# Neighbourhood attention scores as three rounded products of keys and queries that are split on arrival

## The chip, the cores and the metric

One core of one Trainium2 chip runs the whole kernel as one program. The metric is device time in microseconds. Three runs of the kernel before took 1056.29, 1057.15 and 1058.18 us; the median is 1057.15 us.

## The reference

One layer of an encoder over 2048 tokens, which form a grid of 32 rows by 64 columns, with 1024 features and 16 heads of 64. The tokens are normalised (RMS), projected to queries, keys, values and a gate, and each token attends to a window of 8 rows by 16 columns around it, with a learned bias for each relative position. Gated outputs are projected, added to the input and normalised again.

```python
h = rmsnorm(x, norm_0)
q, k, v, gate = jnp.split(h @ w_in_0, 4, axis=-1)
# each row r, blocks of 16 query columns, 8 key rows and 32 key columns around them:
s = jnp.einsum('bnqhd,bknjhd->bhnqkj', qr, kr).astype(jnp.float32) * scale
s = jnp.where(col_valid[None, None], s + bias[None], NEG_INF)
p = jax.nn.softmax(s.reshape(B, H, nb, NA_QBLOCK, kh * NA_KBLOCK), axis=-1)
o = jnp.einsum('bhnqkj,bknjhd->bnqhd', p, vr)
x = x + (o * silu(gate)) @ w_out_0
return rmsnorm(x, norm_f)
```

All inputs are float32.

## The kernel before

The kernel first computes most projections (stages one and two, lines 570 to 907), to about 582 us of the profile. Every one of their products is made of three matmuls with operands in a rounded float32 format (F32R): an operand is split into a rounded high part, copied by ACT (ScalarE), and the remainder, subtracted by DVE (VectorE); the product is high x high + high x low + low x high, added up in PSUM.

Then the attention runs in 33 steps m (line 1429). A step's unit is a pair of heads p and a group T of eight query rows; `order` (line 933) has first the eight pairs with T = 0, then sixteen steps with T = 1 and 2, then eight with T = 3. The number of key rows of T = 0 to 3 is 11, 15, 15 and 12 (`KEY_ROWS`), so the key tile kt holds 704, 960, 960 or 768 columns of 64; the queries qt hold 512. The two heads of the pair lie in partitions 0 to 63 and 64 to 127.

The order of all instructions is written out by hand (`manual_schedule`), and every engine works through its own list in that order. One step m emits:

1. `begin` (line 1404) queues loads for later points of the step on SP (SyncE): the gate sgt for unit m-1 (`load_sg`, pool sp, two buffers), the values of unit m, the queries and keys of unit m+1 (`load_q`, `load_k`, two buffers each).
2. `feed(8)`: eight matmuls of what is left of the projections or, later, of the output projection (lines 379 to 383, 1346 to 1350). `feed` also emits stores and other work that has come due.
3. `normalise(2m-1)` (line 1044): a reciprocal on DVE (L1046), then the probabilities of half a unit are scaled, two tiles by GpSimd (L1055) and two by ACT (L1053).
4. One set of roots of finished output rows (`run_roots`, eight small DVE operations, L1248 to L1255), the splitting of rows for the output projection (`split_rows`, L1198 on ACT, L1199 on DVE) or of weights (`consume`, L189 and L190, L194 and L195), and the rest of the step's feed.
5. `turns(m-1)` (line 1078): PE (TensorE) transposes the probabilities of unit m-1 into six PSUM banks (L1112), and ACT and DVE copy three banks each to SBUF (tile pta, L1088).
6. `scores(2m)` and `scores(2m+1)` (line 1016): for each of four column groups and two heads one float32 matmul of queries and keys (L1027), DVE adds bias and mask from tile em and takes the row minimum (L1035), and ACT does Exp with the row sum (L1041).
7. `values(2m-2)`, `values(2m-1)` (line 1117): PE multiplies pta by the values into bank o (L1134), and DVE multiplies by the gate (L1140).

All PSUM tiles rotate through eight banks. In the first step there is nothing to normalise, and `feed(a * 0.6)` follows `feed(8)` directly.

A 128 x 128 tile `ones` is set by DVE at the start, copied by ACT into the rounded `onesr` (line 674), and read by one GpSimd instruction (line 1466) that only makes that engine wait for pta. `ident`, an identity matrix made by GpSimd, serves the transposes.

Of the kernel before, what the change touches and what calls it, by code (L numbers as in the profile page):

```python
# [10 lines left out]
F32 = mybir.dt.float32  # L11
F32R = mybir.dt.float32r
BF16 = mybir.dt.bfloat16
I32 = mybir.dt.int32
AF = mybir.ActivationFunctionType
OP = mybir.AluOpType
# [4 lines left out]
ROWS, GW, KH, KW = 32, 64, 8, 16  # L21
# [12 lines left out]
KEY_ROWS = [(0, 11), (4, 19), (12, 27), (20, 32)]  # L34
# [36 lines left out]
def build(ctx, tc, x, xr, xt, wg, rpb, last, w_out, n0, nf, masks, out):  # L71
    nc = tc.nc
# [8 lines left out]
    def pool(name, bufs):  # L81
        p = ctx.enter_context(tc.tile_pool(name=name, bufs=bufs))
        return lambda shape, dt, nm: p.tile(shape, dt, name=nm, tag=name)
# [3 lines left out]
    wp = pool("wp", 8)  # L87
    raw = pool("raw", 6)
    kp = pool("kp", 2)
    qp = pool("qp", 2)  # L90
    vp = pool("vp", 2)
    vhalf = []
# [4 lines left out]
            vhalf.extend((t[:, :512], t[:, 512:]))  # L97
        return vhalf.pop(0)

    sp = pool("sp", 2)  # L100
    xp = pool("xp", 8)
    mkp = pool("mkp", 1)
    pt = pool("pt", 1)
    mp = pool("mp", 10)
# [19 lines left out]
        nc.tensor.matmul(zp, z[:, :128], z, start=True, stop=True)  # L124
    ident = one.tile([128, 128], F32, name="ident")
    make_identity(nc, ident)
    ones = one.tile([128, 128], F32, name="ones")
    nc.vector.memset(ones, 1.0)
    onesr = one.tile([128, 128], F32R, name="onesr")
    rt = one.tile([128, 16], F32, name="rt")  # L130
    rth = one.tile([128, 8], F32, name="rth")
# [438 lines left out]
    def stage_one():  # L570
# [6 lines left out]
        land["x12"] = [kp([128, 960], F32, "land")[:, :512] for _ in range(2)] + [xp([128, 512], F32, "land") for _ in range(2)]  # L577
        sixth = sixths()
        land["x21"] = [spot[:, k] for k in range(3)] + [lp([128, 512], F32, "land")]
        slots = [(mp, 512)] * 8 + [(sp, 512)] * 2 + sixth[:2] + [(vh, 512)] * 4  # L580
        slots += sixth[2:] + [(mp, 512)] * 2 + [(qp, 512)] * 2

        def load(f, k):
# [87 lines left out]
        parts_ = slice(0, 256), slice(256, 512)  # L671
        load_v0(0, 0, 0, cols=parts_[0], by=nc.scalar)
        load_x(0, "x11", 0, land["x11"][0], parts_[0])
        nc.scalar.activation(onesr, ones, AF.Copy)
        load_v0(0, 1, 0, cols=parts_[0])
        load_x(0, "x11", 0, land["x11"][0], parts_[1])
        load_v0(0, 0, 0, cols=parts_[1])
# [120 lines left out]
    def stage_two():  # L798
# [3 lines left out]
        for k in range(4):  # L802
            load_x(2, "x22", k, x22[k])
        slots = {"T2": [(mp, 512)] * 8,
                 "T3": [(sp, 512)] * 2 + sixth[:5] + [(lp, 512)],
                 "T4": [(vh, 512)] * 4 + [(mp, 512)] * 2 + [sixth[5], (qp, 512)]}

        def also(n, i):
# [120 lines left out]


    KT, VT, QT, EM, SG, E = {}, {}, {}, {}, {}, {}
    LAST, stored_at = {}, {}
    order = [(p, 0) for p in range(NP)] + [(p, T) for p in range(NP) for T in (1, 2)] + [(p, 3) for p in range(NP)]
    pairs = [(p, T, (h, h + 1)) for p, T in order for h in (0, 2)]
# [9 lines left out]
    def load_k(p, T):  # L944
        r0, r1 = KEY_ROWS[T]
        n = (r1 - r0) * GW
        must(*[("k", p, c) for c in range(r0 // 8, (r1 + 7) // 8)])

        def keys():
            t = kp([128, 960], F32, "kt")  # L950
            KT[p, T] = t.rearrange("p (r c) -> p r c", c=GW)
            nc.sync.dma_start(t[:, :n], kd[p][:, r0 * GW:r1 * GW])

        return keys

    def load_q(p, T):
        must(("q", p, T))
# [58 lines left out]
    def scores(i, between=None):  # L1016
        p, T, cs = pairs[i]
        kt, qt = KT[p, T], QT[p, T]
        r0, r1 = KEY_ROWS[T]
        got = []  # L1020
        for C in cs:
            c0, c1 = KEY_COLS[C]
            qs = slice(C * 128, C * 128 + 128)
            pst = [bank((r1 - r0) * (c1 - c0), f"s{s}") for s in range(2)]
            for s in range(2):
                a = slice(s * 64, s * 64 + 64)
                nc.tensor.matmul(pst[s], qt[a, qs], kt[a, :r1 - r0, c0:c1].rearrange("p r (s c) -> p s r c", c=8), start=True, stop=True)  # L1027
            got.append((C, pst))
        ST[i] = st = tiny.tile([128, 12], F32, name="st")
        for j, (C, pst) in enumerate(got):  # L1030
            n = (r1 - r0) * width(C)
            X[i, C] = [xp([128, 512], F32, f"x{s}")[:, :n] for s in range(2)]
            for s in range(2):
                o = 2 * j + s
                nc.vector.tensor_tensor_reduce(X[i, C][s], pst[s], EM[p, ROW_TYPE[T], COL_TYPE[C], s], -1.0, 1e38,  # L1035
                                               OP.add, OP.min, st[:, o:o + 1])
            if between and j == 0:
                between()
            for s in range(2):
                o = 2 * j + s  # L1040
                nc.scalar.activation(X[i, C][s], X[i, C][s], AF.Exp, bias=st[:, o:o + 1], scale=-1.0,  # L1041
                                     accum_out=st[:, 4 + o:5 + o])
# [386 lines left out]
    for m in range(cycles + 1):  # L1429
        a = amount[m] - 8  # L1430
        begin(m)
        feed(8)
        if m:
            due_here = []
            quiet[0] = True
            if a < 12 and m > 8 and m % 2:
                normalise(2 * m - 1, True, lambda: due_here.append(split_rows() or consume(1, turn=True)))
            else:
                normalise(2 * m - 1, True)
            if a > 12:  # L1440
                run_roots()
            elif not rows_due():
                run_roots(1)
            for k in range(3):
                if m == 1 and k == 2:
                    pass
                elif a > 12 or not any(due_here) and (k < 1 or k < 2 and m > 8 and m % 2 == 0):
                    got = split_rows()
                    due_here.append(got)
                    if not got:  # L1450
                        consume(1, turn=True)
                    elif a < 12 and m % 2 == 0 and len(items) - state["used"] == 8:
                        feed(a * 0.2)
                        consume(1, turn=True)
                feed(a * 0.2)
        else:
            feed(a * 0.6)
        quiet[0] = False
        feed(a * 0.4, 8 if a > 12 else 4)
        sums = next_sums(m) == m + 1  # L1460
        if m:
            turns(m - 1)
            first_sums = m + 2 if m + 2 in pair_steps else m + 1 if sums and m + 1 not in pair_steps else None
            if first_sums:
                after = tiny.tile([128, 12], F32, name="st")
                nc.gpsimd.tensor_scalar(after[:88, 0:1], PT[m - 1][:88, 1, 0:1], ones[:88, 0:1], 1.0, op0=OP.mult, op1=OP.mult)
                tables(first_sums, 0, 1)
        if m == cycles:
            all_loads()
            feed(6)  # L1470
        else:
            scores(2 * m)
            if sums:
                tables(m + 1, 2)
            if m == 0:
                feed(first)
            scores(2 * m + 1, lambda: normalise(2 * m))
            if m == 0:
                consume(2, turn=True)
        if m:  # L1480
            values(2 * m - 2)
            values(2 * m - 1)
        runs[0] += 1
        for n in range(2, 24):
            if n < 8 and m == n - 2 or n == 8 and m == 5 or n in pair_steps and m == n - 3:
                for f in load_e(order[n][0], ROW_TYPE[order[n][1]], homes=accs if n >= 8 and n % 4 == 0 else None):
                    f()
        if m == 20:
            late_loads()
# [52 lines left out]
```

## Time and profile before

| | us |
|---|---|
| median of three runs | 1057.15 |
| lowest, highest | 1056.29, 1058.18 |
| span of the profiled execution | 1054.4 |
| PE busy | 1046.1 |
| DVE busy | 696.7 |
| ACT busy | 537.2 |
| GpSimd (POOL) busy | 252.0 |

The profile gives one execution by its span, from the first to the last instruction; no separate time of that execution is known, and the median of the runs lies 2.75 us above the span. A row of a group names the line, the engine, the operation, output and inputs, shapes and count; then the busy time, the mean duration of one in ns, and the idle time of the engine before such an instruction with what ended it. A row of a timeline begins with start and duration in us. Durations overlap a little with the next instruction on the same engine, so prices are better taken from one start to the next.

### The profile page before, as it was taken

The numbers are of one execution on the slowest core, as the hardware profiler recorded it, in microseconds if no ns is written. First come the engines' busy times: TensorE is split into PE (matmuls) and PEld (weight loads), VectorE is DVE, ScalarE is ACT, GpSimd is POOL, SyncE is SP. The second block draws the span as 40 slices with busy tenths as digits, with TensorE's granted clock in tenths as the row PEclk, the third lists the DMA queues.
The fourth block names the chain that finished last, engine by engine and source line by source line (L and its number), as shares of the span: only waits on it lengthen the run. The fifth ranks groups of instructions, "written<-read, shape, count | busy, mean of one in ns | idle before, by whom it ended". The sixth has DMA issues, their size and how long they took to land.

```text
span 1054.4 us, 20160 instructions
## 1 busy us (share of the span) xinstructions
PE 1046.1 (99%) x7316; PEld 858.8 (81%) x7316; DVE 696.7 (66%) x1570; ACT 537.2 (51%) x1260; POOL 252.0 (24%) x342
## 2 busy tenths in 40 slices
PE   9999999999999999999999999999999999999997
PEld 7888888887888888888888788888887888888886
DVE  5476667778897625555655766687777886667554
ACT  7645223443444334232332677688787865455422
POOL 0000322312211000000002467666665322112100
PEclk9999999999999999999999999999999999999999
DMA  9634444343635433333236777778777588775352
GB/s 320 219 100 118 132 150 136 120 144 120 187 119 154 121 100 93 116 110 121 90 110 211 219 232 235 219 252 281 243 237 217 184 277 272 245 233 183 120 166 80
DMA packets 120252, 184.19 MB, mean 175 GB/s; under 512 B 10776, under 2 KB 55064, under 8 KB 120152
## 3 DMA queue, kind: packets, MB, share of 16 engines
q1 hardware_dynamic: 119720, 182.50, 55.1%
q8 instruction: 57, 0.93, 0.4%
q10 hardware_dynamic: 432, 0.40, 0.1%
q14 instruction: 43, 0.35, 0.1%
HBM read 132.53 MB, written 50.33 MB: 173 GB/s over the span
## 4 chain that ended last, share of the span: by engine, by line
PE 96%; DVE 2%; issue 1%; ACT 1%; DMA 0%; SPq 0%; DVEq 0%; ACTq 0%
PE pp L435 36%; PE pv L559 17%; PE s L1027 8%; PE o L1134 8%; PE po L1346 6%; PE po L1348 5%; PE po L1350 5%; PE ph L1112 4%; PE pp L381 2%; PE pp L383 2%; PE pp L379 2%; DVE f L418 0%; DVE x L1035 0%; DMA raw<-in_wg_dram 0%; DVE raw L424 0%
## 5 line engine op out<-in xcount | busy, mean ns | idle before, releaser
L435 PE MATMUL pp<-h,f 128*128 128x512 f32 x672 | 217.4, 389 | 0.0
L1041 ACT ACTIVATE x<-x,st 128x360 f32<-128x360 f32 (+5 forms) x256 | 151.1, 592 | 23.0 <-DVE st L1035 23.0
L1055 POOL TENSOR_SCALAR x<-x,st 128x480 f32<-128x480 f32 (+5 forms) x192 | 111.7, 599 | 153.5 <-DVE st L1046 148.6
L435 PEld LDWEIGHTS pp<-h,f 128*128 128x128 f32 x672 | 126.2, 188 | 26.2
L435 PE MATMUL pp<-t,f 128*128 128x512 f32 x558 | 141.7, 389 | 0.1
L435 PE MATMUL pp<-l,f 128*128 128x512 f32 x336 | 130.7, 389 | 0.0
L1035 DVE CUSTOM_DVE_ANT_0 x<-s,em 128x360 f32<-128x360 f32 (+5 forms) x256 | 123.0, 535 | 0.5 <-PE s L1027 0.4
L435 PEld LDWEIGHTS pp<-t,f 128*128 128x128 f32 x558 | 104.7, 188 | 22.2 <-DVE u L448 0.6
L455 POOL TENSOR_TENSOR tmp<-tmp,rb 128x512 f32<-128x512 f32 x36 | 58.4, 1622 | 268.3 <-DVE tmp L453 232.8
L995 POOL TENSOR_TENSOR em<-e,mk 128x264 f32<-128x264 f32 (+3 forms) x64 | 50.8, 825 | 259.8 <-PE pp L435 246.3
L418 DVE TENSOR_TENSOR f<-raw,f 128x512 fp32r<-128x512 f32 x105 | 76.5, 729 | 43.6 <-ACT f L417 43.5
L1346 PE MATMUL po<-woh,gh 128*128 128x512 f32 x252 | 99.8, 396 | 0.1
L1348 PE MATMUL po<-woh,gl 128*128 128x512 f32 x252 | 98.7, 391 | 0.0
L1350 PE MATMUL po<-wol,gh 128*128 128x512 f32 x252 | 98.6, 391 | 0.0
L1027 PE MATMUL s<-kt,q 64*128 64x480 f32 (+5 forms) x512 | 94.6, 487 | 0.0
L1134 PEld LDWEIGHTS o<-pta,vt 120*64 120x64 f32 (+2 forms) x1792 | 80.9, 137 | 13.9 <-DVE st L1035 13.6
L559 PE MATMUL pv<-wh,h 128*128 128x512 f32 x256 | 88.3, 390 | 0.0
L559 PE MATMUL pv<-wl,h 128*128 128x512 f32 x256 | 88.2, 390 | 0.2 <-DVE wl L542 0.2
L559 PE MATMUL pv<-wh,l 128*128 128x512 f32 x256 | 88.2, 389 | 0.0
L1088 DVE COPY pta<-ph 120x512 f32<-120x512 f32 (+5 forms) x96 | 56.9, 639 | 43.5 <-PE ph L1112 43.3
L1134 PE MATMUL o<-pta,vt 120*64 120x128 f32 (+5 forms) x1792 | 85.3, 253 | 0.0
L1027 PEld LDWEIGHTS s<-kt,q 64*128 64x128 f32 x512 | 64.9, 186 | 15.3 <-DVE pta L1088 1.3
(156 smaller groups left out, 1705.3 us busy)
## 6 DMA issues: line engine op xcount, KB each, us to landing
raw<-in_wg_dram SPq DMA_DIRECT2D x124, 256.0 KB, 4.3
row<-in_xr_dram SPq DMA_DIRECT2D x32, 256.0 KB, 4.1
vd<-v SPq DMA_DIRECT2D x32, 256.0 KB, 2.5
sgd<-sg SPq DMA_DIRECT2D x32, 256.0 KB, 2.4
q<-qd SPq DMA_DIRECT2D x32, 256.0 KB, 5.2
sgt<-sgd SPq DMA_DIRECT2D x32, 256.0 KB, 4.9
xr<-in_x_dram SPq DMA_DIRECT2D x32, 256.0 KB, 3.8
ogd<-og SPq DMA_DIRECT2D x32, 256.0 KB, 2.7
```

Source lines behind the costliest of these rows:

```text
L418: nc.vector.tensor_tensor(t[:, 1], src, t[:, 0].bitcast(F32), OP.subtract)
L435: nc.tensor.matmul(B[n, P], t[:, int(m == 2), c], x[k][int(m == 1)], start=P in (1, 6, 5) and k == 0 and m == 0, stop=k == 3 and m == 2, s ...
L455: nc.gpsimd.tensor_tensor(tmp, tmp, rb[c], OP.mult)
L559: nc.tensor.matmul(ps[t], a[:, o], b, start=k == 0 and m == 0, stop=k == NK - 1 and m == 2)
L1027: nc.tensor.matmul(pst[s], qt[a, qs], kt[a, :r1 - r0, c0:c1].rearrange("p r (s c) -> p s r c", c=8), start=True, stop=True)
L1035: nc.vector.tensor_tensor_reduce(X[i, C][s], pst[s], EM[p, ROW_TYPE[T], COL_TYPE[C], s], -1.0, 1e38, OP.add, OP.min, st[:, o:o + 1])
L1041: nc.scalar.activation(X[i, C][s], X[i, C][s], AF.Exp, bias=st[:, o:o + 1], scale=-1.0, accum_out=st[:, 4 + o:5 + o])
L1055: nc.gpsimd.tensor_scalar(X[i, C][s], X[i, C][s], st[:, o:o + 1], 1.0, op0=OP.mult, op1=OP.mult)
L1134: nc.tensor.matmul(to.rearrange("d (h q) -> d h q", q=64) if nq > 64 else to, vt[:k, strip, s * 64:s * 64 + 64], t[:k, h, at:at + 64] if n ...
L1346: nc.tensor.matmul(p, gh, woh[q, j], start=(i == 0), stop=False)
L1348: nc.tensor.matmul(p, gl, woh[q, j], start=False, stop=False)
L1350: nc.tensor.matmul(p, gh, wol[q, j], start=False, stop=(i == NK - 1))
```

## The change

Keys and queries of each unit are split when they have arrived: ACT copies each into a rounded high part (kh in a new pool khp with one buffer, qh in pool lp, which has one buffer), and DVE subtracts, so that the old tiles hold the low parts. Each float32 matmul of `scores` becomes three F32R matmuls that add up in the same bank, high x high, high x low and low x high, with the two heads alternating within each round. The split stands behind `normalise` and ahead of the roots and the other splits of the step; in the first step it stands ahead of the second feed. All four row groups T are split. The pool sp has one buffer instead of two, and the places where earlier stages borrowed its second buffer borrow the tile of khp. The tile `ones` is gone: onesr is made from ident by scale 0 and bias 1, and the GpSimd instruction reads ident.

```diff
+    khp = pool("khp", 1)
...
-    sp = pool("sp", 2)
+    sp = pool("sp", 1)
...
-    ones = one.tile([128, 128], F32, name="ones")
-    nc.vector.memset(ones, 1.0)
...
-        slots = [(mp, 512)] * 8 + [(sp, 512)] * 2 + sixth[:2] + [(vh, 512)] * 4
+        slots = [(mp, 512)] * 8 + [(sp, 512), (khp, 960)] + sixth[:2] + [(vh, 512)] * 4
...
-        nc.scalar.activation(onesr, ones, AF.Copy)
+        nc.scalar.activation(onesr, ident, AF.Copy, scale=0.0, bias=1.0)
...
-                 "T3": [(sp, 512)] * 2 + sixth[:5] + [(lp, 512)],
+                 "T3": [(sp, 512), (khp, 960)] + sixth[:5] + [(lp, 512)],
...
+    KH, QH = {}, {}
+    SPLIT = (0, 1, 2, 3)
...
+    def split_kq(p, T):
+        n = (KEY_ROWS[T][1] - KEY_ROWS[T][0]) * GW
+        kt, qt = KT[p, T].rearrange("p r c -> p (r c)"), QT[p, T]
+        kh, qh = khp([128, 960], F32R, "kh"), lp([128, 512], F32R, "qh")
+        nc.scalar.activation(kh[:, :n], kt[:, :n], AF.Copy)
+        nc.vector.tensor_tensor(kt[:, :n].bitcast(F32R), kt[:, :n], kh[:, :n].bitcast(F32), OP.subtract)
+        nc.scalar.activation(qh, qt, AF.Copy)
+        nc.vector.tensor_tensor(qt.bitcast(F32R), qt, qh.bitcast(F32), OP.subtract)
+        KH[p, T], QH[p, T] = kh.rearrange("p (r c) -> p r c", c=GW), qh
...
-            for s in range(2):
-                a = slice(s * 64, s * 64 + 64)
-                nc.tensor.matmul(pst[s], qt[a, qs], kt[a, :r1 - r0, c0:c1].rearrange("p r (s c) -> p s r c", c=8), start=True, stop=True)
+            terms = [(qt, kt)]
+            if T in SPLIT:
+                qh, kh, ql, kl = QH[p, T], KH[p, T], qt.bitcast(F32R), kt.bitcast(F32R)
+                terms = [(qh, kh), (qh, kl), (ql, kh)]
+            for n, (q, k) in enumerate(terms):
+                for s in range(2):
+                    a = slice(s * 64, s * 64 + 64)
+                    nc.tensor.matmul(pst[s], q[a, qs], k[a, :r1 - r0, c0:c1].rearrange("p r (s c) -> p s r c", c=8),
+                                     start=n == 0, stop=n == len(terms) - 1)
...
+            if m < cycles and order[m][1] in SPLIT:
+                split_kq(*order[m])
             if a > 12:
                 run_roots()
...
         else:
+            split_kq(*order[0])
             feed(a * 0.6)
...
-                nc.gpsimd.tensor_scalar(after[:88, 0:1], PT[m - 1][:88, 1, 0:1], ones[:88, 0:1], 1.0, op0=OP.mult, op1=OP.mult)
+                nc.gpsimd.tensor_scalar(after[:88, 0:1], PT[m - 1][:88, 1, 0:1], ident[:88, 0:1], 1.0, op0=OP.mult, op1=OP.mult)
```

## The prediction

> **What bounds the kernel now.** I read the page first, then the stages, then the chain of waits, then single steps.
>
> ```profile
> span 1054.4 us, 20160 instructions
> PE 1046.1 (99%) x7316; PEld 858.8 (81%) x7316; DVE 696.7 (66%) x1570; ACT 537.2 (51%) x1260; POOL 252.0 (24%) x342
> ...
> PE 96%; DVE 2%; issue 1%; ACT 1%; DMA 0%; SPq 0%; DVEq 0%; ACTq 0%
> ```
>
> Over the whole span PE is never idle and the chain that ends last runs on PE for 96% of it, so PE time saved is time gained, as long as nobody else is late. But the shares are means. The change acts in the attention steps alone, from about 584 us on, and these come in three kinds (row types 0, then 1 and 2, then 3; eight, sixteen and eight steps). The windows view (width, then PE, PEld, DVE, ACT, POOL busy, with counts):
>
> ```profile
> 598.24:671.65 73.41, 73.41 (x930) 60.44 (x929) 47.69 (x163) 54.72 (x161) 53.97 (x91) 1.00 0.80 237
> 671.65:848.98 177.33, 177.22 (x2121) 143.98 (x2121) 134.99 (x401) 143.55 (x377) 100.66 (x145) 1.00 0.73 229
> 848.98:1054.40 205.42, 198.92 (x1646) 164.75 (x1645) 128.06 (x373) 92.98 (x256) 26.05 (x48) 0.99 0.61 199
> ```
>
> In the middle stage, sixteen steps of 177.33/16 = 11.1 us, ACT is busy 143.55 us (81%) and DVE 134.99 us (76%): 9.0 and 8.4 us of a step. That is where new ACT and DVE work must show. In the last stage they have room.
>
> **What PE saves.** The scores of a step, in the chain of waits (start, us, matmuls), one step of each kind:
>
> ```profile
> 620.77 2.42 PE s L1027 x15
> ...
> 705.80 3.00 PE s L1027 x16
> ...
> 907.41 2.56 PE s L1027 x15
> ```
>
> A run of rounded (F32R) matmuls shows the streaming rate:
>
> ```profile
> 565.76 2.88 PE L435 MATMUL pp<-t,f 128*128 128x512 f32 x12
> ```
>
> (2.88 - 0.39)/11 = 0.226 us for 512 columns, one round: 2.26 columns per ns. A middle step has 360+480+480+360 = 1680 score columns per head. Four rounds with the two heads side by side make 4 x 1680/2.26 = 2.97 us, and the row has 3.00: the float32 product costs four rounds, and both heads share the time. Three rounds cost 2.23, so PE saves 0.74 us in a middle step; with 1232 and 1344 columns it is 0.55 and 0.59 in the others. Over all 32: 8 x 0.55 + 16 x 0.74 + 8 x 0.59 = 21 us. Part of it cannot be had, because the second half of a step's scores needs PSUM banks that the copies of the transposed probabilities (L1088) release:
>
> ```profile
> PEld s L1027 <- DVE pta L1088: 1.3, 5, 0.4
> ```
>
> In steps of types 0 and 3 PE already waits there about 0.25 us; a quicker first half only waits longer. The saving is then that of the second half, 0.3 us; in a middle step about 0.65. On PE alone: 16 x 0.65 + 16 x 0.3 = 15 us.
>
> The Trainium skill ("TensorE: Matmul & The Clock Gate", Part 3, The mechanism) says that a weight load overlaps running matmuls only of another row group; the three rounds load twelve times per head and step instead of eight, so by it the loads would eat the saving. The 3.00 us row speaks against it: it has no room for eight loads beside 2.97 us of streaming. By the page's 128/1.2 = 107 ns a load (an estimate), four more loads would cost 0.43 us where PE sets the pace, in eight steps, and the sum below would be 3 us higher.
>
> **What the splits cost.** split_kq adds per step two ACT copies (kh of 704, 960 or 768 columns, qh of 512) and two DVE subtractions (kl, ql). Similar operations, two in a row, then their slopes by width:
>
> ```profile
> 758.47 1.14 ACT L1198 ACTIVATE gh<-ograw 128x512 fp32r<-128x512 f32 x2
> ...
> 759.12 1.29 DVE L1199 TENSOR_TENSOR gl<-ograw,gh 128x512 fp32r<-128x512 f32 x2 [1.67 <-ACT gh L1198]
> ```
>
> ```profile
> L1041 ACT ACTIVATE x<-x,st 128x480 f32<-128x480 f32 x64 | 43.5, 681 | 0.0
> ...
> L1041 ACT ACTIVATE x<-x,st 128x360 f32<-128x360 f32 x64 | 37.4, 585 | 11.6 <-DVE st L1035 11.6
> ...
> L1199 DVE TENSOR_TENSOR gl<-ograw,gh 128x512 fp32r<-128x512 f32 x30 | 19.6, 691 | 6.3 <-ACT gh L1198 6.1
> ...
> L1199 DVE TENSOR_TENSOR gl<-ograw,gh 128x384 fp32r<-128x384 f32 x2 | 1.1, 553 | 0.0
> ```
>
> From start to start 0.52 us on ACT and 0.60 on DVE for 512 columns; (681-585)/120 = 0.80 ns a column on ACT, (691-553)/128 = 1.08 on DVE. A middle step: kh 0.89, qh 0.52, kl 1.07, ql 0.60, that is 1.41 on ACT and 1.67 on DVE. Busy sums alone: ACT 9.0 + 1.4 = 10.4, DVE 8.4 + 1.7 = 10.1, against a PE step of 11.1 - 0.65 = 10.4. It would just fit, if order allowed. It does not. One light middle step, ACT and DVE:
>
> ```profile
> 746.60 0.18 DVE L1046 RECIPROCAL st<-st 128x4 f32<-128x4 f32 x1 [0.40 <-ACT x L1041]
> 746.81 1.08 ACT L1053 ACTIVATE x<-x,st 128x360 f32<-128x360 f32 x2 [0.24 <-DVE st L1046]
> ...
> 748.22 0.60 ACT L359 ACTIVATE sg<-pp 128x512 f32<-128x512 f32 x1 [0.32 <-PE pp L383]
> ...
> 748.85 0.69 DVE L360 SCALAR_TENSOR_TENSOR sg<-sg,pp 128x512 f32<-128x512 f32 x1 [2.07 <-ACT sg L359]
> ...
> 749.83 1.78 DVE L1088 COPY pta<-ph 120x512 f32<-120x512 f32 x3 [0.29 <-PE ph L1112]
> 751.52 0.52 DVE L1035 CUSTOM_DVE_ANT_0 x<-s,em 128x360 f32<-128x360 f32 x1
> ...
> 752.09 0.59 ACT L1041 ACTIVATE x<-x,st 128x360 f32<-128x360 f32 x1 [0.71 <-DVE st L1035]
> ```
>
> Both engines take their work in program order. The split stands behind normalise(2m-1), so kh waits on ACT until the last Exp, the reciprocal and the two scalings of L1053 are done (747.80). kl on DVE waits for kh. Behind kl and ql on DVE stand this step's roots, row splits and weight splits, then the three copies of L1088, then the first masked minimum (751.52), which releases the first Exp (752.09). It is one loop through the step, and the split lies in it: kh 0.89, handing over 0.13, kl 1.07, ql 0.60, together 2.69 us from 747.80 on, then sg 0.60: the copies could start at 751.1 instead of 749.83. This step grows by 1.3 us, and PE, which would come 0.65 earlier, waits for banks and for pta. The gap between the end of L1053 and the first DVE copy was 2.0 us here; what is to go into it is 2.69 plus whatever DVE does behind the split.
>
> That remainder, over the sixteen steps (groups of the window from 672 to 849), and the roots of one late step, first and last of eight:
>
> ```profile
> L1088 DVE COPY pta<-ph 120x512 f32<-120x512 f32 (+3 forms) x48 | 28.6, 641 | 10.6 <-PE ph L1112 10.5
> L195 DVE TENSOR_TENSOR wol<-raw,woh 128x512 fp32r<-128x512 f32 x16 | 11.6, 747 | 11.0 <-ACT woh L194 11.0
> ...
> L1199 DVE TENSOR_TENSOR gl<-ograw,gh 128x512 fp32r<-128x512 f32 x8 | 5.3, 700 | 4.6 <-ACT gh L1198 4.6
> ```
>
> ```profile
> 846.43 0.18 DVE L1248 TENSOR_SCALAR st<-st 128x1 f32<-128x1 f32 x1
> ...
> 848.48 0.16 DVE L1255 SCALAR_TENSOR_TENSOR st<-st 128x1 f32<-128x1 f32 x1
> ```
>
> Twelve of the 16 wol, six of the 8 gl, and seven other full-width operations stand behind the split, 25 x 0.62 = 15.5 us, and two sets of roots of 2.1: 19.8 us, or 1.24 a step. So 2.68 + 1.24 = 3.92 us must go into a gap that the timelines of the sixteen steps show as 2.05 in the mean (2.0 in the step above): +1.87 us a step, **+29.8 us** in the middle stage (0.5 in the lightest steps, 4.1 and 3.4 in the two with roots, which today run while DVE would wait). DVE idle before those 48 copies is 10.6 us in all, the only cover there was.
>
> Type 0 steps, one of seven:
>
> ```profile
> 616.87 0.93 ACT L1053 ACTIVATE x<-x,st 128x264 f32<-128x264 f32 x2 [0.24 <-DVE st L1046]
> ...
> 620.11 1.75 DVE L1088 COPY pta<-ph 88x512 f32<-88x512 f32 x3 [1.07 <-PE ph L1112]
> ```
>
> Free at 617.70, copies at 620.11: a gap of 2.41. New: kh 0.68, handing over 0.13, kl 0.80, ql 0.60, one weight split 0.60 = 2.81, +0.4 here; the seven sum to **+2.1**, two of them on PE's pace. Type 3 steps have room (width, PE, PEld, DVE busy):
>
> ```profile
> 868.27:887.27 19.00, 19.00 (x172) 15.82 (x174) 11.93 (x36) 9.61 (x27) 3.26 (x6) 1.00 1.03 340
> ```
>
> DVE is busy for 11.93 of 19.00 us, so the split hides behind the projections that PE works on; PE's 0.3 is gained eight times: **-2.4**. If that cover were gone it would cost up to 1.4 us each.
>
> The first step has no cover. scores(0) came from whole tiles; now it waits for the split behind the rest of stage two:
>
> ```profile
> 584.21 1.31 PE L1027 MATMUL s<-kt,q 64*128 64x264 f32 x8
> ```
>
> ```profile
> 586.64 1.52 DVE L360 SCALAR_TENSOR_TENSOR sg<-sg,tmp 128x512 f32<-128x512 f32 x2
> 588.08 0.43 DVE L1035 CUSTOM_DVE_ANT_0 x<-s,em 128x264 f32<-128x264 f32 x1
> ```
>
> DVE is free for kl at 588.1, ql ends about 589.6, where the scores began at 584.2. PE stands in order and waits some 5 us, of which the late DVE of step 1 gives a little back: **+4.2**.
>
> DVE subtractions slow down while POOL works: L195 above has 747 ns against 691. At 8% of 1.67 us in 23 steps: **+3**. The upper bound is this pair of one operation:
>
> ```profile
> L424 DVE TENSOR_TENSOR raw<-raw,s 128x512 f32<-128x512 f32 x21 | 26.5, 1260 | 0.0
> ...
> L424 DVE TENSOR_TENSOR raw<-raw 128x512 f32<-128x512 f32 x21 | 14.4, 685 | 0.0
> ```
>
> a factor of 1.84, or 1.4 us in each step while POOL is busy (57% of the middle stage): 18 us more.
>
> Edits at nothing: the matrix of ones (one memset of DVE in the first microseconds; onesr now waits for ident, which POOL makes well before the first weights land); the identity in the gate at L1466. One buffer of sp instead of two: the load of sgt, today issued a step ahead, waits in SP's queue for og, ahead of the store of og and the loads of v, q and k; one issue of some 0.6 us, against landings that are several microseconds early. If it were late, og would be late by the landing, a few microseconds a step; I take nothing.
>
> The sum against the profiled span: 29.8 + 2.1 - 2.4 + 4.2 + 3 = +36.7, 1054.4 to 1091. The median of the runs, 1057.15, lies 2.75 above the span; I leave that as it is: **1094 us**.
>
> **Rivals.**
> - *The split fits in the slack* and PE stays the pace: the 15 us of PE are gained, 1057 - 15 = 1042. For it: busy sums just fit (10.4 against 10.4). Against it: the loop above. It decides if the gap between L1053 and the copies takes the split, which 2.05 us do not. 7%.
> - *Only ACT paces*, with kl and ql hidden beside it. The idle of ACT before its copies in the middle stage:
>
> ```profile
> L1088 ACT ACTIVATE pta<-ph 120x512 f32<-120x512 f32 (+3 forms) x48 | 25.0, 559 | 14.4 <-PE ph L1112 13.9
> ```
>
>   The step grows by 1.41 less 14.4/16 = 0.9, that is 0.5 in sixteen steps, plus 4.2 for step 0, less 2.4: +10, 1067. Against it: the copies of DVE stand behind ql. 12%.
> - *POOL slows every subtraction*, or sgt comes late: 1112. 12%.
> - *The change does not do what it says*: heads or loads of weights run one after the other, and three rounds take as long as four. In the first 24 steps it hides in the waits; type 3 pays about 1 us, +8, 1102. The rows of 3.00 us speak against it. 3%.
>
> **How the numbers follow.** Forecast 66%, 1094, from 1075 to 1106 by itself. The range runs from the ACT case to the POOL case, 1066 to 1110; outside are the first rival and some of the third. Faster 0.07; within 0.2% (2 us, about what a measurement of this kernel can tell) 0.02; slower 0.91.
>
> The skill's same page (Part 1) says that PE's clock halves after an idle window of about 3.4 us; the profile grants full clock where PE never waits, and no run here shows such waits, so by it at most some steps with 4 us of waiting would add a microsecond or two each.
>
> **What would show it.** Right: a step of the middle stage near 13 us; the score matmuls at three quarters of their time; DVE busy nearly without a break from kl to the first minimum; PE idle ended by pta copies of DVE (L1088) for 30 us or more; type 3 steps a little shorter; about 5 us of PE idle before the first scores. Wrong: middle steps at or under 11.1 us, or PE waits that end with ACT, with sgt, or with the loads of k.

## The result, and the profile after

The changed kernel takes 1093.77 us (median of four runs, 1093.16 to 1095.80); the kernel before took 1057.13 us beside it. The ratio is 1.0352, with a 95% interval of 1.0339 to 1.0365: 3.5% slower. The profiled execution has a span of 1091.3 us, 36.9 more than before. From the page of the changed kernel:

```profile
span 1091.3 us, 20860 instructions
PE 1059.8 (97%) x7572; PEld 873.4 (80%) x7572; DVE 740.3 (68%) x1633; ACT 576.0 (53%) x1324; POOL 251.6 (23%) x342
...
PEclk9999999999999999999998999999999989999999
```

PE is busy for 97% instead of 99%, DVE has 44 us more work and ACT 39. The row of the granted clock has an 8 in two of its 40 slices; before, it was 9 throughout. Where the time went is seen in the windows view, cut in both kernels at the first Exp of step 0, of step 1, of step 8, of step 24 and of step 31 (the stretches are one step, seven of type 0, sixteen of types 1 and 2, seven of type 3). Before:

```profile
588.55:601.73 13.18, 13.18 (x102) 9.90 (x101) 9.33 (x28) 9.81 (x28) 6.23 (x11) 1.00 0.89 255
601.73:674.66 72.93, 72.93 (x929) 60.51 (x928) 46.59 (x162) 53.80 (x159) 54.07 (x92) 1.00 0.80 235
674.66:852.64 177.98, 177.87 (x2126) 143.89 (x2123) 136.41 (x404) 144.08 (x379) 99.21 (x143) 1.00 0.73 229
852.64:984.24 131.60, 131.60 (x1186) 109.63 (x1185) 86.35 (x258) 68.89 (x194) 22.79 (x42) 1.00 0.74 240
```

After:

```profile
591.30:610.62 19.32, 18.41 (x126) 14.36 (x124) 10.89 (x30) 11.24 (x29) 6.22 (x11) 0.90 0.57 166
610.62:685.78 75.16, 73.92 (x986) 62.65 (x985) 56.86 (x176) 62.17 (x172) 54.14 (x92) 1.00 0.76 228
685.78:890.45 204.67, 187.77 (x2249) 151.60 (x2247) 159.78 (x436) 163.45 (x412) 99.28 (x143) 0.98 0.66 201
890.45:1021.62 131.17, 131.17 (x1246) 111.55 (x1245) 93.86 (x272) 77.55 (x207) 22.78 (x42) 0.99 0.71 233
```

The first number after the window is its width. The middle stage grew by 26.7 us, the first step by 6.1, and the first Exp came 2.75 later; the type 0 steps cost 2.2, the type 3 steps and the rest gave back 0.9. A middle step now takes 204.67/16 = 12.8 us instead of 11.1. One of them, the same light step whose rows the prediction shows, in the timeline after:

```profile
765.67 0.18 DVE L1063 RECIPROCAL st<-st 128x4 f32<-128x4 f32 x1 [0.85 <-ACT x L1058]
...
765.88 1.08 ACT L1070 ACTIVATE x<-x,st 128x360 f32<-128x360 f32 x2 [0.25 <-DVE st L1063]
...
766.87 0.99 ACT L961 ACTIVATE kh<-kt 128x960 fp32r<-128x960 f32 x1
...
767.89 1.16 DVE L962 TENSOR_TENSOR kt<-kt,kh 128x960 fp32r<-128x960 f32 x1 [2.04 <-ACT kh L961]
...
768.97 0.68 DVE L964 TENSOR_TENSOR q<-q,qh 128x512 fp32r<-128x512 f32 x1
...
769.57 0.68 DVE L359 SCALAR_TENSOR_TENSOR sg<-sg,pp 128x512 f32<-128x512 f32 x1
770.16 1.74 DVE L1105 COPY pta<-ph 120x512 f32<-120x512 f32 x3
```

ACT is free at 766.87, and kh starts at that moment. DVE waits 2.04 us for it and then has kl, ql and the gate's product ahead of the copies of pta (L1105). From the reciprocal to the copies it is now 4.49 us; it was 3.23. The waits view of the changed kernel, from 605 to 882 us (total, times, longest):

```profile
DVE kt L962 <- ACT kh L961: 42.4, 23, 3.3
ACT x L1058 <- DVE st L1052: 38.4, 21, 3.7
...
PEld s L1043 <- DVE pta L1105: 11.7, 20, 1.4
...
PE s L1043 <- DVE pta L1105: 5.4, 11, 1.0
```

DVE waits for kh, the Exps (L1058) wait for the minima (L1052) behind it, and PE and its weight loads wait for the copies. PE's transposes, which ended the longest waits ahead of the copies before, no longer stand among the long waits of this stretch: DVE now comes later than PE.

### The profile page after: what moved, and what is told of

Its sections match the earlier page's. It is cut to its first block, busy times and chain, and to the rows that moved or that the text cites. A ratio compares the mean times of both kernels' runs of the same rounds, so it can differ in the third digit from the quotient of the medians.

```text
span 1091.3 us, 20860 instructions
## 1 busy us (share of the span) xinstructions
PE 1059.8 (97%) x7572; PEld 873.4 (80%) x7572; DVE 740.3 (68%) x1633; ACT 576.0 (53%) x1324; POOL 251.6 (23%) x342
## 5 line engine op out<-in xcount | busy, mean ns | idle before, releaser
L1058 ACT ACTIVATE x<-x,st 128x360 f32<-128x360 f32 (+5 forms) x256 | 151.2, 593 | 47.3 <-DVE st L1052 47.2
L1052 DVE CUSTOM_DVE_ANT_0 x<-s,em 128x360 f32<-128x360 f32 (+5 forms) x256 | 123.0, 534 | 6.1 <-PE s L1043 6.0
L1043 PE MATMUL s<-kh,qh 64*128 64x360 f32 (+5 forms) x256 | 73.8, 414 | 22.0 <-ACT qh L963 6.0
L416 ACT ACTIVATE f<-raw 128x512 fp32r<-128x512 f32 x105 | 63.7, 624 | 26.5 <-PE pp L434 10.4
L434 PEld LDWEIGHTS pp<-l,f 128*128 128x128 f32 x336 | 63.1, 188 | 13.1
```

Of the source, the lines that this page charges most:

```text
L416: nc.scalar.activation(t[:, 0], src, AF.Copy)
L434: nc.tensor.matmul(B[n, P], t[:, int(m == 2), c], x[k][int(m == 1)], start=P in (1, 6, 5) and k == 0 and m == 0, stop=k == 3 and m == 2, s ...
L1043: nc.tensor.matmul(pst[s], q[a, qs], k[a, :r1 - r0, c0:c1].rearrange("p r (s c) -> p s r c", c=8), start=n == 0, stop=n == len(terms) - 1)
```

## The experiments

All times below are medians; ratios are against the kernel before on the same chip. Step lengths are taken from first Exp to first Exp.

**1. Are the edits at nothing really at nothing?** The pools, the identity and the single sgt buffer stay, the split and the rounds go:

```diff
-    SPLIT = (0, 1, 2, 3)
+    SPLIT = ()
...
-            split_kq(*order[0])
```

> The edits around the change alone: one buffer of sp, the pool khp, onesr made from ident; no split, float32 scores as before. My theory (the split's DVE work stands in a loop through each step) prices these edits at nothing: 1057 us, within 1.5 us, middle steps near 11.1 us. A rival, that the single buffer of sgt holds up SP's queue and with it v, q and k, expects a good part of the 36 us here: 1065 us or more.

1057.00 us, ratio 0.9998 (0.9989 to 1.0007). Everything happens in the split and the rounds; one buffer for sgt costs nothing.

**2. The splits without the rounds.** The low parts go into kh and qh, and the scores stay float32 products of the whole tiles:

```diff
-        nc.vector.tensor_tensor(kt[:, :n].bitcast(F32R), kt[:, :n], kh[:, :n].bitcast(F32), OP.subtract)
+        nc.vector.tensor_tensor(kh[:, :n], kt[:, :n], kh[:, :n].bitcast(F32), OP.subtract)
...
-        nc.vector.tensor_tensor(qt.bitcast(F32R), qt, qh.bitcast(F32), OP.subtract)
+        nc.vector.tensor_tensor(qh, qt, qh.bitcast(F32), OP.subtract)
...
-                terms = [(qh, kh), (qh, kl), (ql, kh)]
```

> The splits are made as in the changed kernel, with the same four operations at the same places, but the low parts go to waste (they overwrite the high parts) and the scores are float32 products of the whole tiles. My theory: the copies of the transposed probabilities still stand behind both subtractions on DVE, so the middle steps stay near 12.8 us and the stages of rows 0 to 2 lose 27 to 29 us; only the wait of the first scores goes, about 8 us of it: 1086 to 1089 us. A rival, that the three rounds on PE or their wait for the low parts are the loss, expects 1057 to 1062 us.

1092.03 us, ratio 1.0326 (1.0307 to 1.0346). The middle stage grew by 26.9 us, as in the changed kernel, step by step. So the loss comes from the four operations of the split, and with them in place it makes no difference to the middle stage whether PE does four rounds or three. The time is 3 us above what was expected: the wait that left the first step turned up in the second, as in run 9, and the step at the border to type 3 is 2.3 us longer, behind a stretch at half clock from 883 to 890 us.

**3. The rounds without the splits.** Three rounds of the unsplit tiles, read as rounded:

```diff
-                qh, kh, ql, kl = QH[p, T], KH[p, T], qt.bitcast(F32R), kt.bitcast(F32R)
-                terms = [(qh, kh), (qh, kl), (ql, kh)]
+                terms = [(qt.bitcast(F32R), kt.bitcast(F32R))] * 3
...
-            if m < cycles and order[m][1] in SPLIT:
-                split_kq(*order[m])
...
-            split_kq(*order[0])
```

> Three rounded rounds per score product, without any split: all three rounds multiply the unsplit keys and queries, so the scores are not the reference's; the work of PE is that of the changed kernel. My theory: PE sets the pace again and gains 0.65 us in each of the sixteen middle steps and 0.2 to 0.3 in the other sixteen, 13 to 15 us: 1042 to 1044 us. A rival, that weights or heads do not overlap in three rounds, expects no gain: 1055 to 1060 us.

1051.98 us, ratio 0.9946 (0.9931 to 0.9961). The most that PE could give is 5 us, not 15: 0.17 us in the mean of the middle steps and 0.15 in that of type 3. Both sides of the expectation missed. The score products themselves show why. The light middle step, before and then with three rounds:

```profile
749.83 1.78 DVE L1088 COPY pta<-ph 120x512 f32<-120x512 f32 x3 [0.29 <-PE ph L1112]
750.36 3.17 PE L1027 MATMUL s<-kt,q 64*128 64x360 f32 x16
...
753.00 0.08 DVE L1035 DVE_READ_ACCUMULATOR2_ANT st<- 128x1 f32 x1
...
753.46 2.67 PE L1134 MATMUL o<-pta,vt 120*64 120x128 f32 x56
```

```profile
747.16 1.78 DVE L1104 COPY pta<-ph 120x512 f32<-120x512 f32 x3 [0.28 <-PE ph L1128]
747.66 3.02 PE L1042 MATMUL s<-kt,q 64*128 64x360 f32 x24
...
750.33 0.08 DVE L1051 DVE_READ_ACCUMULATOR2_ANT st<- 128x1 f32 x1
...
750.61 2.67 PE L1150 MATMUL o<-pta,vt 120*64 120x128 f32 x56
```

From the first score product to the first product of the values (L1134, L1150) PE takes 3.10 us with float32 products and 2.95 with three rounds, without a wait in between. So the rounds save 0.15 us here and not 0.74; in steps of types 0 and 3 it is 0.15 too (2.51 to 2.36, 2.66 to 2.51). How far apart the rounds start is seen where the kernel gives their operands different names, here in a step of type 3 (run 11 below):

```profile
908.95 0.54 PE L1043 MATMUL s<-kh,qh 64*128 64x384 f32 x2
...
909.15 0.53 PE L1043 MATMUL s<-kt,qh 64*128 64x384 f32 x2
...
909.70 0.30 PE L1043 MATMUL s<-kh,qh 64*128 64x288 f32 x1
909.85 0.32 PE L1043 MATMUL s<-kt,qh 64*128 64x288 f32 x1
```

With both heads side by side they start 0.20 us apart for 384 columns and 0.15 for 288, where streaming alone (2.26 columns per ns) would be 0.17 and 0.13; in a middle step of the changed kernel it is 0.25 for 480 columns, where streaming would be 0.21. What a round needs beyond its streaming, no run here takes apart.

A second suspect stood in the waits view of the kernel before: the weight loads of the values wait for DVE's minima, whose banks the values need. In the kernel with three rounds that wait got shorter:

```profile
PEld o L1134 <- DVE st L1035: 10.5, 23, 0.5
```

```profile
PEld o L1150 <- DVE st L1051: 3.5, 13, 0.3
```

In the step above DVE reads its third minimum 3.17 us behind the first copy in both kernels, and the values begin 0.46 us behind that read before and 0.28 with three rounds. So it is not this bank that stops the gain there. In steps of type 3 the values come 0.08 to 0.10 us behind the read, so a quicker PE would soon meet it.

**4 and 5. Which engine paces the loop?** One more copy on ACT, or one more operation on DVE, in each split:

```diff
+        nc.scalar.activation(qh, qt, AF.Copy)
```

> The changed kernel with the ACT copy of the queries (qh) made twice, 0.52 us more of ACT in each step. My theory has DVE in the loop: the second copy ends when kl ends, so nothing waits: 1094 to 1096 us. A rival, that ACT sets the pace of the middle steps, expects 0.52 us in 24 steps: 1104 to 1107 us.

```diff
+        nc.vector.tensor_tensor(qt.bitcast(F32R), qt, qt, OP.max)
```

> The changed kernel with one more pass of DVE over the low part of the queries (a maximum of the tile with itself, which changes nothing), 0.60 us in each step, behind ql. My theory has DVE in the loop of the steps of rows 0 to 2: 0.6 us in 23 steps, 14 us: 1106 to 1109 us. A rival, that ACT sets the pace, expects 1094 to 1096 us.

The ACT copy: 1099.99 us, ratio 1.0404 (1.0388 to 1.0421). The DVE operation: 1114.57 us, ratio 1.0548 (1.0532 to 1.0564). In ordinary middle steps the ACT copy of 0.52 us (start to start) costs 0.11 us, the DVE operation 0.72. In type 0 steps both cost, 0.37 and 0.72. So in the middle DVE paces the loop and ACT comes close behind, closer than the theory had it; both times are 4 to 6 us above the upper end of its ranges. For DVE the rows tell a part of it:

```profile
780.67 0.68 DVE L964 TENSOR_TENSOR q<-q,qh 128x512 fp32r<-128x512 f32 x1
781.39 0.69 DVE L965 TENSOR_TENSOR q<-q 128x512 fp32r<-128x512 f32 x1
782.00 0.68 DVE L359 SCALAR_TENSOR_TENSOR sg<-sg,pp 128x512 f32<-128x512 f32 x1
```

From ql to the next independent operation it is 1.33 us where it was 0.60: an operation that reads the tile just written costs 0.72 from start to start, not 0.60. In 23 steps that is 2.8 us. Stretches in which the granted clock is half (see runs 8 to 10) grew as well: between 580 and 1040 us the clock is at half for 17 us in the changed kernel, for 27 with the ACT copy and for 38 with the DVE operation.

**6. The split ahead of the scalings.** It moves from behind `normalise` to right behind its reciprocal:

```diff
-    def normalise(i, both=False, between=None):
+    def normalise(i, both=False, between=None, first=None):
...
         nc.vector.reciprocal(st[:, 8:12], st[:, 4:8])
+        if first:
+            first()
...
-                normalise(2 * m - 1, True)
-            if m < cycles and order[m][1] in SPLIT:
-                split_kq(*order[m])
+                normalise(2 * m - 1, True, None, arrive)
```

(`arrive` calls `split_kq` under the same condition; the call of `normalise` with `between` has it too.)

> The same work in another order: the split stands right behind the reciprocal of normalise, so ahead of the scalings on ACT and of whatever stands between them; kh then starts with the last Exp and not 1.2 us later, and kl runs while ACT scales. My theory (the place in the loop costs the time) expects middle steps of about 11.6 us instead of 12.8, steps of row 0 at or under their old length, the first step as long as in the changed kernel: 1068 to 1076 us. A rival, that the sums of ACT and DVE work cost the time wherever they stand, expects 1092 to 1095 us.

1079.16 us, ratio 1.0211 (1.0194 to 1.0228). The middle stage grows by 15.5 us instead of 26.7. A light step of it:

```profile
760.53 1.00 ACT L961 ACTIVATE kh<-kt 128x960 fp32r<-128x960 f32 x1
760.67 0.18 DVE L1063 RECIPROCAL st<-st 128x4 f32<-128x4 f32 x1 [0.56 <-ACT x L1058]
...
761.57 1.16 DVE L962 TENSOR_TENSOR kt<-kt,kh 128x960 fp32r<-128x960 f32 x1 [0.72 <-ACT kh L961]
761.95 1.08 ACT L1072 ACTIVATE x<-x,st 128x360 f32<-128x360 f32 x2
...
764.15 1.75 DVE L1107 COPY pta<-ph 120x512 f32<-120x512 f32 x3
```

DVE waits 0.72 us for kh instead of 2.04, and the copies come 3.48 us behind the reciprocal instead of 4.49. What is left of the loss has changed its place: the scalings, for which PE's transposes wait, start 1.28 us behind the reciprocal instead of 0.21. So 11 of the 26.7 us of the middle stage, and 14.6 of the 37 in all, are the place of the split and not its work; the time is 3 us above what was expected.

**7. The roots ahead of the split:**

```diff
-            if m < cycles and order[m][1] in SPLIT:
-                split_kq(*order[m])
             if a > 12:
                 run_roots()
             elif not rows_due():
                 run_roots(1)
+            if m < cycles and order[m][1] in SPLIT:
+                split_kq(*order[m])
```

> The roots stand ahead of the split instead of behind it. My theory: in the two middle steps with roots DVE does them while it would wait for kh, and each step is about 2 us shorter (from 14.2 and 14.5), and the late clock drop with its microsecond may go too: 1088 to 1090 us. A rival, that the roots cost the same wherever they stand, expects 1093 to 1095 us.

1089.56 us, ratio 1.0311 (1.0295 to 1.0326). The two steps with roots take 12.60 and 13.23 us instead of 14.19 and 14.46, and the one behind them 0.9 less. The roots fit into the time in which DVE waits for kh; as expected.

**8 to 10. The first step.** What PE does before the first scores differs (first_fed); the first scores stay float32 products (first_plain); or PE's wait is filled with matmuls that nobody reads (wait_filled).

```diff
+            if m == 0:
+                feed(first)
             scores(2 * m)
...
-            if m == 0:
-                feed(first)
             scores(2 * m + 1
```

> In the first step the sixteen projection matmuls that stood between scores(0) and scores(1) stand ahead of scores(0), so that PE works while the first split is made. If the 8.9 us of the first step are the wait of 4.5 us and the half clock that follows it, PE waits less than 1 us, the clock stays at 1.00, and some 7 us come back: 1086 to 1088 us. If they are the wait alone, without the clock, 3.6 us come back at most: 1090 us or more.

1091.24 us, ratio 1.0330 (1.0315 to 1.0345), no better than the rival said, though PE waits only 0.92 us ahead of the first scores and the clock stays at 1.00 there. What sets the first Exp is then the chain of ACT and DVE through the split. The step behind it is 1.2 us longer than in the changed kernel, with the clock at half from 606.7 to 610.2 us. In its profiled execution the attention also began 2.2 us later than in the kernel before, ahead of the edit, for which no run here shows the reason. By the medians the edit gains 2.5 us.

```diff
-            if T in SPLIT:
+            if T in SPLIT and i > 1:
...
-            split_kq(*order[0])
```

> Only the first unit's scores stay float32 products of unsplit keys and queries; everything else is as changed. Theory (the first step costs 8.9 us: 4.5 us in which PE waits, and the same again in the microseconds behind it, where the records show a granted clock of 0.56): no PE wait ahead of the first scores, clock 1.00 there, about 1085 us. Rival (the step costs the 4.2 us of the prediction, and the low clock is only how the records show the wait): about 1089.5 us.

1091.52 us (1088.24 to 1094.35), ratio 1.0331 (1.0310 to 1.0351): a miss, the theory said 1085. The first step has no wait, and the second has one:

```profile
601.44 0.87 PE L1043 MATMUL s<-kh,qh 64*128 64x264 f32 x2 [1.02 <-ACT k L364]
```

PE's wait of 1.02 us is for a bank that ACT's copy of a projection (L364) releases, and that copy stands on ACT behind the split of step 1 and two copies of weights. The windows view of the same run:

```profile
606.00:615.00 9.00, 9.00 (x63) 7.83 (x60) 3.94 (x12) 5.15 (x15) 4.34 (x8) 0.53 0.48 132
```

PE runs at half its clock for ten microseconds behind that wait. Up to the first Exp of step 2 this kernel is 7.0 us behind the kernel before, the changed one 8.8; and its middle stage is 2.4 us longer than that of the changed one. The lateness of ACT and DVE stays and shows at the next place where PE needs them.

```diff
+            if i == 0 and C == cs[0]:
+                for _ in range(38):
+                    nc.tensor.matmul(pst[0][:, :256], onesr.bitcast(BF16)[:, :128], onesr.bitcast(BF16)[:, :256], start=True, stop=True)
```

> As changed, but ahead of the first scores PE runs 38 matmuls of 256 columns (of the tile of ones, in the bank that the first scores then overwrite; about 0.11 us each, an estimate from 2.26 columns per ns), so that its wait of 4.5 us is filled with work that nobody reads. Theory (half of what the first step loses is the granted clock of 0.50 for 6.8 us behind that wait, which idling brings on): clock 1.00 from 588 to 596 us, the first step 3.4 us shorter, about 1090.4 us. Rival (the step's length is set by the lateness of ACT and DVE alone, and the clock is a consequence that costs nothing): as changed, 1093.8 us; if the matmuls run over the wait, later than that.

1094.03 us (1093.87 to 1094.96), ratio 1.0357 (1.0340 to 1.0375): as changed. Its windows:

```profile
589.00:596.00 7.00, 6.59 (x40) 4.88 (x40) 3.06 (x11) 3.00 (x10) 1.35 (x2) 1.00 0.91 239
743.00:747.00 4.00, 3.52 (x19) 2.86 (x17) 4.00 (x13) 1.83 (x7) 1.71 (x2) 0.57 0.93 312
...
846.00:850.00 4.00, 4.00 (x25) 3.73 (x25) 3.62 (x13) 3.67 (x10) 1.70 (x2) 0.58 0.24 84
873.00:880.00 7.00, 6.78 (x58) 5.90 (x60) 5.43 (x20) 5.14 (x16) 2.28 (x4) 0.52 0.21 73
```

The half of the theory about the place is right: the clock is 1.00 behind the filled wait, and the first step is 2.0 us shorter (not 3.4). The half about the time is wrong: other stretches at half clock came up in the middle stage, at 743 and 846 us, and a longer one at 873, where the changed kernel has none or a shorter one. The middle stage and the steps behind it lost 3.0 us more. Which waits are followed by such a stretch differs from kernel to kernel, where the same rows stand at other times.

**11. Does a part pay?** Only the last seven units of type 3 are split; no other:

```diff
-    SPLIT = (0, 1, 2, 3)
+    SPLIT = (3,)
...
-            if T in SPLIT:
+            if T in SPLIT and p:
...
-            if m < cycles and order[m][1] in SPLIT:
+            if m < cycles and order[m][1] in SPLIT and order[m][0]:
...
-            split_kq(*order[0])
```

> Only the last seven units of the last row group are split and have three rounded products; all other scores are float32 products of unsplit tiles. Theory (PE sets the pace there, and a step gains the 0.2 us that the changed kernel gains in it): 7 x 0.2 = 1.4 us less than before, about 1055.6 us, ratio 0.9987. Rival (the gain of those steps only gives back what the slower steps ahead of them left late): as before, 1057 us, ratio 1.000. Rival (0.3 a step, as the prediction has it): 1055, ratio 0.998.

1055.43 us, ratio 0.9989 (0.9980 to 0.9998), in five rounds: a little faster than before, by 1.1 us. Five of the seven steps are 0.14 to 0.20 us shorter, about the size that run 3 and the changed kernel give. Run 3 apart, whose scores are not the reference's, this is the only version that beats both kernels, and it gains a thousandth.

**12. Do the terms add up?** The middle stage alone is left plain:

```diff
-    SPLIT = (0, 1, 2, 3)
+    SPLIT = (0, 3)
```

> The sixteen units of the row groups 1 and 2 keep float32 products and are not split; the first eight and the last eight units are as changed. Theory (the terms add up: the middle steps cost 26.7 us and about 1 us at each of their ends): middle steps back at 11.1 us, about 1066 us. Rival (part of the middle's cost is lateness that comes out of the first steps and goes on): 1070 us or more.

1068.52 us, ratio 1.0113 (1.0097 to 1.0128). The middle steps are back at 11.1 us, the span is 24.1 us shorter than that of the changed kernel, and the first step costs what it did. The expected 1066 was 2.5 too low: the step at the border to type 3 still is 2.9 us longer. Mostly additive.

## Why the prediction was right, and which terms were off

The time, 1093.77, and the span, 36.9 us longer, are what the prediction said (1094, 36.7). The mechanism is the one it named. That the two numbers meet to a fraction of a microsecond is luck: the middle stage was forecast 6.1 us too long and the other terms together 6.3 too short.

| term of the sum | predicted | measured |
|---|---|---|
| middle stage | +29.8 | +26.7 |
| DVE slowed by POOL | +3 | in the line above, under 1 |
| type 0 steps | +2.1 | +2.2 |
| type 3 steps, and the rest of the span | -2.4 | -0.9 |
| first step | +4.2 | +8.9 |

- **The loop through the middle step** is shown by six runs: the splits alone bring the loss (2), the rounds alone don't (3), an added DVE operation costs its whole length and an ACT copy a fifth of it (4, 5), and the loss falls when kh starts earlier (6) or other DVE work goes into the wait for it (7). The light step was to grow by 1.3 us; it grew by 4.49 - 3.23 = 1.26. The lengths that were estimated by slopes are close; the group of kl in the changed kernel:

```profile
L962 DVE TENSOR_TENSOR kt<-kt,kh 128x960 fp32r<-128x960 f32 x16 | 19.3, 1206 | 29.8 <-ACT kh L961 29.8
```

- **DVE slowed by POOL, +3**, was mis-sized, and the rival *POOL slows every subtraction* falls with it. The mean of 1206 ns above is one long kl among fifteen of 1.16 us:

```profile
679.26 2.17 POOL L1072 TENSOR_SCALAR x<-x,st 128x352 f32<-128x352 f32 x4
680.51 1.92 DVE L962 TENSOR_TENSOR kt<-kt,kh 128x960 fp32r<-128x960 f32 x1 [1.89 <-ACT kh L961]
```

  This kl alone, of 32, met POOL at work, and none of the 32 ql did; it cost 0.8 us. The slowing is real, but in the other steps POOL has ended its scalings when DVE splits, and waits for work from DVE. The prediction took means of groups for the size of the slowing: of the 21 L424 whose mean is 1260 ns, ten take 0.69 us with POOL idle and eleven 1.78 with POOL at work.
- **The first step, +4.2**, was mis-sized by half. The wait was forecast at 5 us and is 4.46 us in the timeline:

```profile
589.08 0.59 PE L1043 MATMUL s<-kh,qh 64*128 64x264 f32 x2 [4.46 <-ACT qh L963]
```

  But nothing of it was given back, the split of step 1 adds 1.3 us (from the transposes to the first Exp 3.49 us before, 4.74 in run 10), and the clock takes 2.0 us (run 10 again). These come to 7.7 of the 8.9 us; the rest was not traced. The term is known to about 1 us, since the first Exp of runs 1 and 3, whose first step is as before, comes at 589.76 and 588.12. The granted clock behind that wait, and behind a wait of the middle stage, in the windows of the changed kernel:

```profile
584.88:588.29 3.41, 0.00 (x0) 0.00 (x0) 2.76 (x5) 2.08 (x4) 0.00 (x0) 1.00 0.75 211
588.29:595.12 6.83, 6.03 (x21) 4.46 (x22) 3.51 (x11) 2.98 (x10) 1.33 (x2) 0.50 0.94 242
793.10:796.51 3.41, 2.44 (x40) 1.76 (x38) 2.61 (x4) 3.01 (x6) 0.00 (x0) 1.00 0.95 284
796.51:799.92 3.41, 3.41 (x22) 2.64 (x20) 3.41 (x12) 1.74 (x5) 1.69 (x2) 0.50 0.81 307
```

  The Trainium skill ("TensorE: Matmul & The Clock Gate", Part 1) has the clock at half or full, switched by windows of about 3.4 us. The trace agrees: the stretch at 796 us is 3.41 us long, the one at 588 twice that, and the one of run 9 three times. The same part of the Trainium skill says that it takes at least one idle window to bring the half clock on. At 588 us that is so, PE is idle for the whole 3.41 us ahead; at 796 us the measurement differs, PE's matmuls are busy for 2.44 of the 3.41 us, and the clock falls all the same. In each trace the stretches begin whole multiples of 3.413 us apart (in the changed kernel at 588.29, 796.51, 875.01 and 888.67 us, that is 61, 23 and 4 of them), so it matters how a wait lies to this beat. Of all runs, 41 such windows between 575 and 1030 us are followed by half clock; PE is busy for 0 to 2.7 us in them, and but for one it does nothing there except transposes and scores. Other windows as little busy are not followed by it (2.07 us at 844 us in the changed kernel); what else decides is open.
- **What PE saves** was mis-sized in every stage: 0.65 us in a middle step and 0.3 in one of type 3 were assumed, the runs show 0.17 in the first and 0.15 to 0.2 in the second (3, 11). The step that failed is the one from four rounds to three: the row of 3.00 us is that of float32 products, and the prediction took three quarters of it for three rounded rounds, which take 2.95 us against 3.10 in run 3. That row also says nothing of the weight loads of rounded rounds (0.19 us each in the trace), which the prediction set aside by it; whether they are what the rounds need beyond streaming is not shown. Nor did PE wait in steps of types 0 and 3 before: the waits of 1.3 us that the prediction read so are of weight loads, beside which the matmuls ran on. It cost the sum little, because in the middle stage nothing of the saving was to be had anyway, but the rival *fits in the slack* would have been 1052 and not 1042.
- Of the signs that the prediction named, the middle step near 13 us, DVE without a break from kl to the first minimum, and the wait ahead of the first scores came. Two did not. The score matmuls' own rows are not at three quarters of their time: between 580 and 1054 us they take 104.55 us, where they took 94.56 before, and 89.77 in run 3, in which they hardly wait. And the rows show PE idle for 204.67 - 187.77 = 16.9 us in the middle stage, and 5.4 us of idle that copies of pta on DVE ended, not 30: the rest of the 26.7 us stands in the rows as PE busy, 9.9 us more of it. Stretches at half clock are a part of that (three of 3.4 us near that stage); how the remainder splits between stretched matmuls and the ends of matmuls, which the profile models, stays open.
- *Only ACT paces* falls by runs 4 and 5, *sgt comes late* by run 1. Of *heads or loads one after the other*, the heads do run side by side, by the starts 0.15 and 0.20 us apart in run 11, where one after the other they would take twice the streaming time. But its premise, three rounds take as long as four, is near the mark (2.95 against 3.10 us), and only the price that it put on this is not.

## What to carry to other kernels

Sums of busy time say whether added work can fit; whether it does fit is decided at the gap into which program order puts it, so write the two engines' rows side by side from the moment the first is free to the moment the next must start, and add the new operations there. Before counting a saving on the bounding engine, measure the new operation by itself, as run 3 does with the rounds alone: the row of another kind of product does not give its price. And where a step makes a busy TensorE wait, even for 0.7 us in 3.4 as in run 7, count the stretch at half clock that may follow.

## What the hardware did that was not expected

- Half clock for 3.4, 6.8 or 10.2 us behind waits of PE as short as 1.02 us (run 9), and behind a window of 3.41 us with PE busy for 2.7 of it (run 7, 869.65 to 873.06 us), at places that changed from kernel to kernel; in the kernel before and in run 11, where PE hardly waits, there was no such stretch between 570 and 1050 us. The four executions of run 9 spread over 6.1 us with mean granted clocks of 0.986 to 0.990, the two of the lower clocks being the longer ones; the eleven of run 11 spread over 0.9 us.
- Two dependent DVE operations of 512 columns start 0.72 us apart (in all 32 steps of run 5), two independent ones 0.60.
- Rounded rounds with 64 rows and two heads start 0.02 to 0.04 us further apart than their streaming takes, at 288 to 480 columns, while float32 products of 480 columns, two heads as well, start 0.80 us apart, 0.05 less than four times 480 columns at 2.26 per ns. So three rounds save 0.15 us a step against the float32 products, where 0.55 to 0.74 were computed.
- A DVE subtraction of 960 columns that met GpSimd at work took 1.92 us instead of 1.16.
